# First loads of a hybrid decoder step put on one DMA queue in small pieces, and the square root's activation table loaded behind a square

## The chip, the cores and the metric

The kernel runs on one core of a Trainium2 chip. A core has five engines that run side by side, each with an instruction queue of its own: TensorE (PE, with its weight loads shown as PEld), VectorE (DVE), ScalarE (ACT), GpSimd (POOL) and SyncE (SP, which only issues transfers). ACT and POOL can issue transfers too; each issuing engine has a DMA queue, and all queues run on the same 16 DMA engines. The metric is the device time of one execution in microseconds (us), lower is better.

## The reference, cut to what matters

The reference is one layer of a hybrid decoder for 256 prompt tokens and 8 x 8 sample tokens (320 in all, width 2048), in fp32:

```
h    = rms_norm(x, norm_mix_pre)
proj = h @ w_in                                  # 2048 x 9248
a_u, a_v, z, xbc, dt_raw = split(proj)
gate = chunk_spatial_gate(a_u, a_v, ...)         # gelu, layer norm, masked 128x128 mix per head
ssm  = ssd_mixer(z, xbc, dt_raw, ...)            # causal conv, silu, chunked state space scan, group rms norm
x    = x + rms_norm(concat(gate, ssm) @ w_out, norm_mix_post)
up   = causal_conv(rms_norm(x, norm_ffn_pre) @ ffn_w_up)
x    = x + rms_norm((gelu_tanh(g) * u) @ ffn_w_down, norm_ffn_post)    # g, u = halves of up
```

with `rms_norm(x, w) = x * rsqrt(mean(x*x) + 1e-6) * w`. The new convolution and state-space states are outputs as well.

## The kernel before

All activations are kept with the model width on the 128 partitions and the 320 tokens along the free dimension: x is `xT`, 16 k-tiles of 128 x 320, behind 16 columns that hold the first norm's weights.

**Matmuls.** Each weight block is split into a rounded part `whi` and a rest `wlo`, and each activation into `h_hi` and `h_lo`; `accumulate` (L126) makes three matmuls of them, 128 x 128 by 128 x 320 each: hi x hi, hi x lo, lo x hi. `slab` (L110) loads a piece of a weight matrix into `wraw` on SP's queue (L115), casts it to `whi` on ACT (L117) and subtracts on DVE (L119) to make `wlo`. `wraw`, `whi` and `wlo` have three buffers each, so the load of a slab waits until the third slab before it has been split, and a cast waits until TensorE is done with the third slab before it.

**project** (L152) multiplies the 2048 rows of a weight matrix by 512 (or 256) of its columns. Its list `cuts` runs over the k-tiles: with `small=4` the first four slabs hold one k-tile x 512 columns (256 KB), the next four hold two k-tiles (512 KB), and the last four k-tiles come as two slabs of 256 columns. For each cut it calls `ready(k0, nk)`, if there is one, and then `part`, which calls `slab`, the matmuls and one `tick`. `tick` (L140) advances the background tasks in `bg` by one yield.

**The start.** The first projection (columns V0 to V0 + 511) has `ready=x_ready`. `x_ready` (L525) makes `h_hi` on ACT (L529) and `h_lo` on DVE (L530) from x, scaled by the norm's weights alone: the factor 1/rms, `r1`, is multiplied in when a result leaves PSUM, so the matmuls needn't wait for it. x comes by six transfers that ACT issues ahead of everything (L516 to L518; 1, 1, 2, 4, 4 and 4 k-tiles), with a small square between them (L521) that loads ACT's table early. Before its first real matmul TensorE runs `EARLY` = 10 matmuls of ones (L69).

The sums of squares for `r1` need x once more, with the tokens on the partitions: `load_by_token` (L540) issues six transfers of `x_tok` on POOL's queue, four of 512 KB and two of 256 KB. In front of each, POOL copies one column of `h_hi` of k-tile 8 into the destination, which keeps the transfer behind that k-tile. `x_squares` (L546) squares each piece on ACT with an accumulated sum (L549); each is queued behind one of the last h_hi operations on ACT. The task `with_r1` (L570) has a yield, then `x_squares` and the reciprocal root on DVE, a yield, then `spread` (TensorE turns the column into a row), the parameter loads, and the evacuations `late` of the first projection (`scaled`: DVE multiplies by r1, L334, ACT takes the gelu, L335). It is started once and then advanced by the ticks of the second projection, V0 + 512, 256 columns wide. `turned` (L555) transposes the results on TensorE (`vt_ps`).

**The two later roots.** The mixer's output (`chunk_out(w_out, 7, ...)`, L987) and the FFN's output (`chunk_out(ffn_w_down, g, ...)` with the last g, L1137) are summed up in 16 blocks of 128 x 320. `squares_of` (L284) gives the callback that squares each block as it is finished: blocks 0 to 12 by `add_square` (L276: square on ACT, sum on POOL), 13 to 15 at high priority with the sum on DVE. After the last block `token_sums` adds over the partitions and `rsqrt_by_root` (L237) takes `Sqrt` on ACT (L245), whose table is not the one that gelu, silu and exp use. `root_table` (L252) issues a `Sqrt` of one column whose result nobody reads, so that the table is there beforehand. It is called ahead of each of the two last `chunk_out`s with the last matmul of the chunk before them (L984, L1136).

**Order.** The order of instructions on each engine is set when the program is built, by readiness in a model and by priority: `tc.high_priority(offset=...)` moves what it encloses forward, `first()` being the 200000 step, and a slab's load has 100000. `tc.issue_after(ins)` queues what is traced inside it behind `ins`, as far as it is on the engine of `ins`.

Of the kernel before, what the change touches and what calls it, by code (L numbers as in the profile page):

```python
# [9 lines left out]
F32 = mybir.dt.float32  # L10
F32R = mybir.dt.float32r
I32 = mybir.dt.int32
AF = mybir.ActivationFunctionType
ALU = mybir.AluOpType
# [3 lines left out]
P = 128  # L18
# [3 lines left out]
NT = NP + NS  # L22
D = 2048
KD = D // P
# [1 line left out]
NF = DFF // P  # L26
NH = 32
EPS = 1e-6
EARLY = 10
D_COL = 4 * KD + 120 + 8 * NF  # L30
U0, V0, Z0, X0, B0, C0, DT0 = 0, 2048, 4096, 6144, 8192, 8704, 9216

# [2 lines left out]
def hybrid_step(  # L35
# [10 lines left out]
    act, dve, pool, pe, sp = nc.scalar, nc.vector, nc.gpsimd, nc.tensor, nc.sync  # L46
# [6 lines left out]
    tp = ctx.enter_context(tc.tile_pool(name="tp", bufs=2))  # L53
# [10 lines left out]
    ones = cp.tile([P, P], F32, name="ones")  # L64
# [70 lines left out]
    hT = [None, None]  # L135
# [60 lines left out]
    acc = None  # L196
    pd_last = []
# [54 lines left out]
    def root_table(behind):  # L252

        there = tp.tile([P, 1], F32, name="root_there", bufs=1)
        with tc.issue_after(behind):
            act.activation(there, ones[:, 0:1], AF.Sqrt)
# [18 lines left out]

    def add_square(total, x, begins, adder=pool, place=("sq", 2)):  # L276
        if begins:
            act.activation(total, x, AF.Square)
        else:
            sq = tp.tile([P, NT], F32, tag=place[0], name="sq", bufs=place[1])  # L280
            act.activation(sq, x, AF.Square)
            adder.tensor_tensor(out=total, in0=total, in1=sq, op=ALU.add)

    def squares_of(total):  # L284

        one, held = [], []

        def step(nb):
            if nb < KD - 3:
                add_square(total, acc[:, nb, :], nb == 0)  # L290
                return
            with first():
                if nb < KD - 1:
                    held.append(misc("sq_ps")[:, :NT])
                else:
                    one.append(tp.tile([P, NT], F32, tag="sq", name="sq", bufs=2))
                act.activation((one or held)[-1], acc[:, nb, :], AF.Square)
                if nb > KD - 3:
                    dve.tensor_tensor(out=total, in0=total, in1=held.pop(0), op=ALU.add)
        return step, one  # L300
# [10 lines left out]
    acc = hp.tile([P, KD, NT], F32, name="acc_mix")  # L311
# [50 lines left out]
    with ExitStack() as mctx:  # L362
        op = mctx.enter_context(tc.tile_pool(name="op", bufs=1))
# [138 lines left out]
        with tc.tile_pool(name="gp", bufs=1) as gp:  # L502
# [3 lines left out]
            flat = vt.rearrange("p c d -> p (c d)")  # L506
# [4 lines left out]
            wS = gp.tile([P, 4, NB, TS], F32, name="wS")  # L511
            pool.memset(wS[NS:], 0.0)
            held = gp.tile([P, 1], F32, name="held")
            k = 0
            with tc.high_priority(offset=300000):
                for n in (1, 1, 2, 4, 4, 4):  # L516
                    cs = slice(KD + NT * k if k else 0, KD + NT * (k + n))
                    act.dma_start(flat[:, cs], xT[:, cs])  # L518
                    k += n
                    if k == 2:  # L520
                        act.activation(held, ones[:, 0:1], AF.Square)  # L521

            x_split = []

            def x_ready(k0, nk):  # L525
                with tc.high_priority(offset=100000):
                    for kt in range(k0, k0 + nk):
                        x = xf[:, kt, :]
                        x_split.append(act.activation(hT[0][:, kt, :], x, AF.Copy, scale=pre[:, kt:kt + 1]).ins)  # L529
                        dve.scalar_tensor_tensor(out=hT[1][:, kt, :], in0=x, scalar=pre[:, kt:kt + 1],  # L530
                                                 in1=hT[0][:, kt, :].bitcast(F32), op0=ALU.mult, op1=ALU.subtract)
# [5 lines left out]
            by_tok = [(xp[:, c, D // 2 * i:D // 2 * (i + 1)], slice(0, P), slice(P * c, P * c + P), c, i)  # L537
                      for c in range(2) for i in range(2)]
            by_tok += [(t.rearrange("p k n -> p (k n)")[64:, :D // 2], slice(64, P), slice(NP, NT), 2, i) for i, t in enumerate((bT, cT))]
            def load_by_token():  # L540
                for t, _, rows, c, i in by_tok:

                    pool.tensor_copy(t[:, 0:1], hT[0][:, 8, 0:1][t.shape[0] % P:].bitcast(F32))
                    pool.dma_start(t, x_tok[rows, D // 2 * i:D // 2 * (i + 1)])

            def x_squares():  # L546
                for n, (t, at, _, c, i) in enumerate(by_tok):
# [17 lines left out]

            late = []
            project(w_in, V0, lambda j, ps: scaled(ps, AF.Gelu, vfs[0][:, j, :]), ready=x_ready, small=4, ahead=0, late=late)
            load_by_token()

            def with_r1():  # L570
                yield
                with first():
                    r = x_squares()
                yield
                spread(r, r1)
                params()
                for ev, j, ps in late:
                    ev(j, ps)
# [107 lines left out]
        with tc.tile_pool(name="sd", bufs=1) as sd:  # L686
# [294 lines left out]
            finish(norm3)  # L981
            sq2 = hp.tile([P, NT], F32, tag="ssq", name="sq2")

            root_table(pd_last[-1])  # L984
            bg.append(islice(rest[0], 3))
            squares, one = squares_of(sq2)
            chunk_out(w_out, 7, *res[3], False, squares)  # L987
# [50 lines left out]
    with tc.tile_pool(name="fp", bufs=1) as fp:  # L1038
# [90 lines left out]
        for g in range(NG):  # L1129
            hi, lo = nxt  # L1130
            if g < NG - 1:
                nxt = ffn_up(g + 1)
            if g == 0:
                acc = fp.tile([P, KD, NT], F32, name="acc_ffn")
            if g == NG - 1:
                root_table(pd_last[-1])  # L1136
            chunk_out(ffn_w_down, g, hi, lo, g == 0, last if g == NG - 1 else None)  # L1137

        act.dma_start(o_fconv_p, ptf)
# [125 lines left out]
```

## Time and profile before

| | |
|---|---|
| median of 3 runs | 1821.66 us (1821.31 to 1822.76) |
| span of the profiled execution | 1821.3 us |
| TensorE busy | 1789.4 us, 98% of the span |
| VectorE, ScalarE, GpSimd busy | 1182.3, 798.1, 304.5 us |
| moved by DMA | 294.66 MB, mean 162 GB/s |

The profile is of one execution. Times in it count from the start of the span. A timeline row has the start, the duration, the engine, the line, the operation and what it writes and reads (`out<-in`), with the count of merged operations; in brackets stands the idle time of the engine just ahead of it and what ended it. ACTq, SPq and POOLq are the rows in which an engine issues transfers. Queue q1 is SP's, q10 ACT's and q0 POOL's. Matmuls overlap, so the distance between two starts, not the duration, is what one costs.

### The profile page before, as it was taken

The numbers are of one execution on the slowest core, as the hardware profiler recorded it, in microseconds if no ns is written. First come the engines' busy times: TensorE is split into PE (matmuls) and PEld (weight loads), VectorE is DVE, ScalarE is ACT, GpSimd is POOL, SyncE is SP. The second block draws the span as 40 slices with busy tenths as digits, with TensorE's granted clock in tenths as the row PEclk, the third lists the DMA queues.
The fourth block names the chain that finished last, engine by engine and source line by source line (L and its number), as shares of the span: only waits on it lengthen the run. The fifth ranks groups of instructions, "written<-read, shape, count | busy, mean of one in ns | idle before, by whom it ended". The sixth has DMA issues, their size and how long they took to land.

```text
span 1821.3 us, 31186 instructions
## 1 busy us (share of the span) xinstructions
PE 1789.4 (98%) x12222; PEld 1751.6 (96%) x12222; DVE 1182.3 (65%) x2029; ACT 798.1 (44%) x1102; POOL 304.5 (17%) x626
## 2 busy tenths in 40 slices
PE   8999999999999999999899999999999999999998
PEld 8999999999889899999899999999999999999997
DVE  5449664557977868677776465647465665756575
ACT  6444454334535445444455433333334343433334
POOL 3102200000331312104521010101111010101004
PEclk9999999999999999999999999999999999999999
DMA  8656544455566565556454545444545445454542
GB/s 268 186 150 189 159 132 152 155 157 176 189 192 189 162 196 173 156 159 206 148 149 151 150 153 153 151 152 151 153 152 154 150 154 150 151 148 153 151 154 99
DMA packets 222947, 294.66 MB, mean 162 GB/s; under 512 B 16752, under 2 KB 150736, under 8 KB 222608
## 3 DMA queue, kind: packets, MB, share of 16 engines
q1 hardware_dynamic: 210544, 270.21, 48.6%
q10 hardware_dynamic: 9872, 14.82, 2.2%
q0 software_dynamic: 2384, 7.64, 1.4%
q8 instruction: 96, 1.57, 0.4%
q14 instruction: 51, 0.42, 0.1%
HBM read 277.80 MB, written 14.82 MB: 161 GB/s over the span
## 4 chain that ended last, share of the span: by engine, by line
PE 88%; DVE 4%; DMA 2%; issue 2%; POOL 2%; ACT 1%; ACTq 0%; POOLq 0%; DVEq 0%
PE ps L128 18%; PE ps L130 18%; PE ps L129 18%; PE pd L128 9%; PE pd L130 9%; PE pd L129 9%; DVE wlo L119 1%; PE y_ps L888 1%; DMA cT<-in_x_tok 1%; POOL acc_mix L1023 1%; ACT whi L117 1%; DMA cs<-dacs_d 1%; DMA st<-in_state_ssm 0%; POOL st L808 0%; PE sg L650 0%
## 5 line engine op out<-in xcount | busy, mean ns | idle before, releaser
L119 DVE TENSOR_TENSOR wlo<-wraw,whi 128x1024 fp32r<-128x1024 f32 (+1 forms) x476 | 592.0, 1244 | 455.4 <-ACT whi L117 452.8
L117 ACT CAST whi<-wraw 128x1024 fp32r<-128x1024 f32 (+1 forms) x476 | 496.3, 1043 | 730.2 <-PE ps L129 443.7
L128 PE MATMUL ps<-h_hi,whi 128*128 128x320 f32 x2528 | 787.5, 312 | 8.6 <-ACT whi L117 5.6
L130 PE MATMUL ps<-h_hi,wlo 128*128 128x320 f32 x2528 | 783.9, 310 | 4.3 <-DVE wlo L119 4.3
L129 PE MATMUL ps<-h_lo,whi 128*128 128x320 f32 x2528 | 782.8, 310 | 0.0
L128 PEld LDWEIGHTS ps<-h_hi,whi 128*128 128x128 f32 x2528 | 477.5, 189 | 14.2 <-ACT whi L117 6.9
L130 PEld LDWEIGHTS ps<-h_hi,wlo 128*128 128x128 f32 x2528 | 477.2, 189 | 6.6 <-DVE wlo L119 6.4
L129 PEld LDWEIGHTS ps<-h_lo,whi 128*128 128x128 f32 x2528 | 477.5, 189 | 0.7 <-issue 0.5
L128 PE MATMUL pd<-fhi,whi 128*128 128x320 f32 x704 | 217.0, 308 | 0.0
L129 PE MATMUL pd<-flo,whi 128*128 128x320 f32 x704 | 217.0, 308 | 0.0
L130 PE MATMUL pd<-fhi,wlo 128*128 128x320 f32 x704 | 217.0, 308 | 0.0
L128 PE MATMUL pd<-ohi,whi 128*128 128x320 f32 x448 | 140.8, 314 | 0.0
L129 PE MATMUL pd<-olo,whi 128*128 128x320 f32 x448 | 139.5, 311 | 0.0
L130 PE MATMUL pd<-ohi,wlo 128*128 128x320 f32 x448 | 139.4, 311 | 0.0
L128 PEld LDWEIGHTS pd<-fhi,whi 128*128 128x128 f32 x704 | 132.1, 188 | 0.0
L129 PEld LDWEIGHTS pd<-flo,whi 128*128 128x128 f32 x704 | 132.1, 188 | 0.0
L130 PEld LDWEIGHTS pd<-fhi,wlo 128*128 128x128 f32 x704 | 132.1, 188 | 0.0
L1074 POOL COPY ptf<-pad 128x2 f32<-128x2 f32 x88 | 20.5, 233 | 618.1 <-DVE pad L1062 617.4
L211 DVE TENSOR_TENSOR acc_ffn<-acc_ffn,pd 128x320 f32<-128x320 f32 x160 | 77.5, 484 | 38.7 <-PE pd L130 37.4
L128 PEld LDWEIGHTS pd<-ohi,whi 128*128 128x128 f32 x448 | 84.8, 189 | 2.9 <-issue 1.6
L130 PEld LDWEIGHTS pd<-ohi,wlo 128*128 128x128 f32 x448 | 84.7, 189 | 1.0 <-issue 1.0
L129 PEld LDWEIGHTS pd<-olo,whi 128*128 128x128 f32 x448 | 84.8, 189 | 0.5 <-issue 0.2
(297 smaller groups left out, 1599.4 us busy)
## 6 DMA issues: line engine op xcount, KB each, us to landing
wraw<-in_ffn_w_up SPq DMA_DIRECT2D x176, 512.0 KB, 3.7
wraw<-in_w_in SPq DMA_DIRECT2D x144, 512.0 KB, 3.7
wraw<-in_ffn_w_down SPq DMA_DIRECT2D x88, 512.0 KB, 3.5
wraw<-in_w_out SPq DMA_DIRECT2D x64, 512.0 KB, 3.5
st<-in_state_ssm SPq DMA_DIRECT2D x40, 256.0 KB, 3.8
out_ssm_state_sample<-st ACTq DMA_DIRECT2D x30, 256.0 KB, 3.6
cs<-dacs_d SPq DMA_DIRECT2D x16, 320.0 KB, 4.3
xr<-in_xT SPq DMA_DIRECT2D x4, 640.0 KB, 4.8
```

The source lines that it names most:

```text
L117: act.copy(hi[:, :m], raw[:, :m])
L119: dve.tensor_tensor(out=lo[:, :m], in0=raw[:, :m], in1=hi[:, :m].bitcast(F32), op=ALU.subtract)
L128: pe.matmul(ps, whi, xhi, start=first, stop=False)
L129: pe.matmul(ps, whi, xlo, start=False, stop=False)
L130: return pe.matmul(ps, wlo, xhi, start=False, stop=last).ins
L211: dve.tensor_tensor(out=acc[:, nb, :], in0=acc[:, nb, :], in1=ps[:, :NT], op=ALU.add)
L888: pe.matmul(ps[64 * i:64 * i + 64, cols], w(hl), x(hl, m, cpx), tile_position=(0, 64 * i), **flags)
L1023: added.append((dve if kt < 2 else pool).tensor_tensor(out=a, in0=a, in1=xr[q][:, k, :], op=ALU.add).ins)
L1074: pool.tensor_copy(ptf[:, k, :], pad[:, 256:258])
```

## The change

x is no longer issued by ACT: `x_ready` issues each cut's x on SP's queue, at the priority of the slabs and ahead of the cut's own slab in the text: pieces of 1, 1, 1, 1, 2, 2, 2, 2 and 4 k-tiles. The token loads go to SP as well, one behind the x of k-tile 8, one behind that of 10, two behind that of 12, and the last two behind the first projection; POOL's small copies are gone. `with_r1` has one yield more at its head. `EARLY` is 8.

`add_square` and the callback of `squares_of` now hand over the square's instruction, and the callback calls `root_table` behind the square of block 12 (`nb == KD - 4`), the last that `add_square` makes; the two earlier calls are gone.

```diff
-EARLY = 10
+EARLY = 8
...
     def add_square(total, x, begins, adder=pool, place=("sq", 2)):
         if begins:
-            act.activation(total, x, AF.Square)
-        else:
-            sq = tp.tile([P, NT], F32, tag=place[0], name="sq", bufs=place[1])
-            act.activation(sq, x, AF.Square)
-            adder.tensor_tensor(out=total, in0=total, in1=sq, op=ALU.add)
+            return act.activation(total, x, AF.Square).ins
+        sq = tp.tile([P, NT], F32, tag=place[0], name="sq", bufs=place[1])
+        made = act.activation(sq, x, AF.Square).ins
+        adder.tensor_tensor(out=total, in0=total, in1=sq, op=ALU.add)
+        return made
...
         def step(nb):
             if nb < KD - 3:
-                add_square(total, acc[:, nb, :], nb == 0)
+                made = add_square(total, acc[:, nb, :], nb == 0)
+                if nb == KD - 4:
+                    root_table(made)
                 return
...
-            k = 0
             with tc.high_priority(offset=300000):
-                for n in (1, 1, 2, 4, 4, 4):
-                    cs = slice(KD + NT * k if k else 0, KD + NT * (k + n))
-                    act.dma_start(flat[:, cs], xT[:, cs])
-                    k += n
-                    if k == 2:
-                        act.activation(held, ones[:, 0:1], AF.Square)
+                act.activation(held, ones[:, 0:1], AF.Square)
...
             def x_ready(k0, nk):
                 with tc.high_priority(offset=100000):
+                    cs = slice(KD + NT * k0 if k0 else 0, KD + NT * (k0 + nk))
+                    sp.dma_start(flat[:, cs], xT[:, cs])
+                    for _ in range({8: 1, 10: 1, 12: 2}.get(k0, 0)):
+                        load_by_token()
                     for kt in range(k0, k0 + nk):
...
+            to_load = list(by_tok)
+
             def load_by_token():
-                for t, _, rows, c, i in by_tok:
-
-                    pool.tensor_copy(t[:, 0:1], hT[0][:, 8, 0:1][t.shape[0] % P:].bitcast(F32))
-                    pool.dma_start(t, x_tok[rows, D // 2 * i:D // 2 * (i + 1)])
+                if to_load:
+                    t, _, rows, _, i = to_load.pop(0)
+                    sp.dma_start(t, x_tok[rows, D // 2 * i:D // 2 * (i + 1)])
...
-            load_by_token()
+            with tc.high_priority(offset=100000):
+                while to_load:
+                    load_by_token()
 
             def with_r1():
+                yield
                 yield
...
-            root_table(pd_last[-1])
             bg.append(islice(rest[0], 3))
             squares, one = squares_of(sq2)
             chunk_out(w_out, 7, *res[3], False, squares)
...
-            if g == NG - 1:
-                root_table(pd_last[-1])
             chunk_out(ffn_w_down, g, hi, lo, g == 0, last if g == NG - 1 else None)
```

## The prediction

> **What bounds the kernel now.** I read the page first (busy shares, chain of waits), then windows over the start, then the timeline of each engine at the start and at the two places where a square root is taken.
>
> ```profile
> span 1821.3 us, 31186 instructions
> PE 1789.4 (98%) x12222; PEld 1751.6 (96%) x12222; DVE 1182.3 (65%) x2029; ACT 798.1 (44%) x1102; POOL 304.5 (17%) x626
> PE 88%; DVE 4%; DMA 2%; issue 2%; POOL 2%; ACT 1%; ACTq 0%; POOLq 0%; DVEq 0%
> ```
>
> TensorE is busy for 98% of the span and carries 88% of the chain. A change that leaves its work alone can win only where it idles or runs slowly, so I looked for those places inside the stages that are edited. The windows have the columns length, then busy time and count of PE, PEld, DVE, ACT and POOL, then granted clock, DMA share, GB/s.
>
> ```profile
> 5.70:42.25 36.55, 31.98 (x194) 30.02 (x195) 20.41 (x39) 25.23 (x41) 9.14 (x16) 0.95 0.89 285
> ...
> 26.00:29.21 3.21, 3.21 (x14) 3.21 (x13) 0.55 (x2) 2.28 (x5) 0.00 (x0) 0.50 1.08 206
> 42.25:56.67 14.42, 14.42 (x102) 14.40 (x101) 8.03 (x10) 8.98 (x14) 4.67 (x8) 1.00 0.71 206
> ```
>
> The first projection has 16 k-tiles x 4 blocks x 3 = 192 matmuls. From 42.25 TensorE runs without a gap: about 96 matmuls and a few transposes in 14.42 us, so 0.147 us each, or 28.2 us for 192. The first 192 took from 5.72 to about 42.1, 36.4 us: **8.2 us are lost** after the first matmul. The rows below show where.
>
> ```profile
> 1.13 4.54 PE L70 MATMUL early<-ones 128*128 128x128 f32 x20 [1.13 <-DVE ones L66]
> ...
> 5.72 0.41 PE L128 MATMUL ps<-h_hi,whi 128*128 128x320 f32 x1
> ```
> ```profile
> 11.40 0.31 PE L130 MATMUL ps<-h_hi,wlo 128*128 128x320 f32 x1
> 12.77 0.41 PE L128 MATMUL ps<-h_hi,whi 128*128 128x320 f32 x1 [1.07 <-ACT whi L117]
> ```
> ```profile
> 22.61 0.31 PE L130 MATMUL ps<-h_hi,wlo 128*128 128x320 f32 x1
> 24.47 0.41 PE L128 MATMUL ps<-h_hi,whi 128*128 128x320 f32 x1 [1.55 <-ACT whi L117]
> 24.72 0.31 PE L129 MATMUL ps<-h_lo,whi 128*128 128x320 f32 x1
> 25.73 0.48 PE L130 MATMUL ps<-h_hi,wlo 128*128 128x320 f32 x1 [0.70 <-DVE wlo L119]
> ```
>
> Start to start, the gap at 12.77 costs 1.37 - 0.15 = 1.2 us, the one at 24.47 costs 1.86 - 0.15 = 1.7, the one at 25.73 costs 1.01 - 0.15 = 0.9. Behind them the granted clock is 0.50 for 3.2 us: some 13 matmuls at 0.27 instead of 0.147, 1.6 us. These are 5.4 of the 8.2; the rest is handed over in pieces of 0.1 to 0.7 us while hi and lo halves are made.
>
> Who is late at 12.77 and 24.47? Rows of SP's issues, of the queues' shares at 7.7 to 9.0, of landing times, and of ACT:
>
> ```profile
> 1.73 0.43 SPq L115 DMA_DIRECT2D wraw<-in_w_in  x1
> 6.42 0.33 SPq L115 DMA_DIRECT2D wraw<-in_w_in  x1
> ```
> ```profile
> q10 hardware_dynamic: 116, 0.54, 100.5%
> ```
> ```profile
> wraw<-in_w_in SPq DMA_DIRECT2D x1, 256.0 KB, 5.6
> ```
> ```profile
> 22.33 1.06 ACT L549 ACTIVATE acc_mix<-acc_mix 128x1024 f32<-128x1024 f32 x1 [4.98 <-DMA acc_mix<-in_x_tok]
> 23.29 0.19 ACT L549 ACTIVATION_READ_ACCUMULATOR acc_mix<-acc_mix 128x1 f32 x1
> 23.39 1.03 ACT L117 CAST whi<-wraw 128x1024 fp32r<-128x1024 f32 x1
> ```
>
> The fourth slab is issued at 6.42 (raw slabs have three buffers) and lands 5.6 us later, since ACT's queue, q10, holds all of the engines with x that is needed much later. At 22.33 ACT has stood 4.98 us for x by token, which POOL fetched, and the cast that TensorE needs stands behind that square. Both are what an order of loads can cure.
>
> **The change part by part.** *Loads.* Six transfers of x leave ACT's queue and become nine, six token loads leave POOL's; all go to SP, between the slabs. The bytes stay: x 320 x 2048 x 4 = 2.62 MB, the same again by token, weights 2048 x 512 x 4 = 4.19 MB. Can one queue carry it, and soon enough?
>
> ```profile
> 2.50:14.00 11.50, 10.05 (x57) 9.06 (x56) 6.87 (x15) 7.66 (x16) 2.97 (x15) 1.00 1.02 403
> 14.00:18.00 4.00, 3.63 (x25) 3.37 (x24) 3.76 (x6) 3.35 (x6) 3.94 (x8) 1.00 0.66 182
> 18.00:33.00 15.00, 12.75 (x75) 12.22 (x74) 4.29 (x6) 8.31 (x13) 1.64 (x4) 0.89 1.01 287
> 36.50:38.70 2.20, 1.72 (x12) 1.46 (x10) 2.06 (x7) 2.14 (x5) 0.21 (x1) 1.00 1.08 396
> ```
>
> From 36.50 on only SP's queue has work (the slab and the parameters), and it moves 396 GB/s; two queues moved 403. An issue takes SP about 0.4 us (1.73 row), so fifteen more take 6 us of a sequencer that is otherwise waiting. In the order of use a k-tile costs (160 + 256) KB = 0.426 MB, 1.06 us at 403 GB/s, against 12 x 0.147 = 1.76 us of TensorE. With the four token loads placed among them, all that must land before the first of the last two slabs is used is 2.62 + 2.10 + 3.67 = 8.39 MB: 2.5 + 8.39/0.403 = 23.3 us, plus about 1.0 for the cast, 24.3. TensorE would want it at 4.9 + 12 x 1.76 = 26.0. It fits, with 1.7 us to spare. The x pieces now stand behind slabs that wait for a raw buffer; a buffer comes free when its lo half is made, long before TensorE needs the x of three slabs later, so I count nothing for that. Left over I put 0.6 us for the first halves, 0.3 for other hand-overs and 1.0 for a slab that arrives late: 1.9 of the 8.2, so **-6.3 us**. The bounds are 0 (all of it comes back) and -8.2 (none).
>
> *The first matmul.* The ten warm-up matmuls take 4.54 us, 0.454 each; eight end at 1.13 + 3.63 = 4.76. Today the first cast ends at 5.67 behind two transfers (x on ACT's queue, the slab on SP's) that share the engines with their successors. With x and slab first on one queue, 424 KB need 1.05 us at 403 GB/s, behind a start at about 2.5; ACT then needs about 1.1 for h_hi and the cast, 4.7. I take 4.9: **-0.8 us**, bounds 0 and -0.95.
>
> *POOL.* Six small copies and six issues go; POOL is idle before and behind them in that stretch, so 0.
>
> *One more yield.* The spread of r1 and the four late evacuations come one slab later, 24 x 0.147 = 3.5 us.
>
> ```profile
> 54.03 1.19 ACT L335 ACTIVATE vf<-ev 128x320 f32<-128x320 f32 x3
> ```
> ```profile
> 56.51 1.47 PE L561 MATMUL vt_ps<-ident,vf 128*128 128x128 f32 x12
> ```
>
> The last of these gelus ends at 55.22 and the transposes that read them start at 56.51: 1.3 us of cover. One slab later they would be 2.2 us late, if the transposes keep their place. But the order of an engine is made by readiness:
>
> ```profile
> 4.87 0.10 POOL L594 MEMSET mv<- 128x6 f32 x1
> ```
>
> This memset stands in the text behind four projections and runs at 4.87. Matmuls of the next projection can go first in the same way, so I take 0 and keep +2.2 for the range.
>
> *The square root's table.* Today the helper asks to be put behind a matmul, an instruction of another engine, and what it issues is on ACT:
>
> ```profile
> 36.89 1.28 ACT L256 ACT_TABLE_LOAD   x1
> 38.18 0.44 ACT L256 ACTIVATE root_there<-ones 128x1 f32<-128x1 f32 x2
> ```
>
> Both dummies ran at 38.2, long before a root. The real roots then loaded again:
>
> ```profile
> 857.39 1.28 ACT L245 ACT_TABLE_LOAD   x1
> ...
> 858.29 0.16 DVE L244 SCALAR_TENSOR_TENSOR rs_v<-tsum,rs_v 128x3 f32<-128x3 f32 x1 [0.44 <-PE tsum L263]
> 858.68 0.20 ACT L245 ACTIVATE rs_s<-rs_v 128x3 f32<-128x3 f32 x1
> ```
> ```profile
> 1804.43 0.56 ACT L1125 ACTIVATE acc_ffn<-acc_ffn,prm 128x320 f32<-128x320 f32 x1
> ...
> 1805.01 1.28 ACT L245 ACT_TABLE_LOAD   x1
> ...
> 1805.32 0.16 DVE L244 SCALAR_TENSOR_TENSOR rs_v<-tsum,rs_v 128x3 f32<-128x3 f32 x1 [1.17 <-PE tsum L263]
> 1806.31 0.20 ACT L245 ACTIVATE rs_s<-rs_v 128x3 f32<-128x3 f32 x1
> ```
>
> Behind a square, an ACT instruction, the dummy holds its place, and no gelu, silu or exp stands between it and the root. At the end the operand is ready at 1805.48 and the root starts at 1806.31; without the load it starts at about 1805.52: **-0.8**. In the middle: 858.45 to 858.68, **-0.2**. The load moves to 1.28 + 0.2 = 1.5 us after the square of block 12:
>
> ```profile
> 1798.65 0.47 ACT L281 ACTIVATE sq<-acc_ffn 128x320 f32<-128x320 f32 x1 [0.69 <-DVE acc_ffn L211]
> ...
> 1800.35 0.44 ACT L297 ACTIVATE sq_ps<-acc_ffn 128x320 f32<-128x320 f32 x1 [0.63 <-DVE acc_ffn L211]
> ```
>
> That ends at 1800.6, so the next square is 0.3 late; the scaled copies are pushed too, and the last square (1803.9) comes 3 us later, time enough. Without this cover the load would cost its 1.3 us again. The load at 36.89 goes for nothing gained; TensorE's next wait is for a lo half whose cast (ACT, just ahead of the load) was done by then:
>
> ```profile
> 38.76 0.41 PE L130 MATMUL ps<-h_hi,wlo 128*128 128x320 f32 x1 [0.54 <-DVE wlo L119]
> ```
>
> The Trainium skill, "ScalarE: Activation LUTs", section "What ACT_TABLE_LOAD costs", gives a switch as 1.28 us of load plus 1.38 us of drain, which by estimate would make the two gains together up to 2.8 larger, 1810.8 in all. Here the load starts 0.02 us after the operation before it and the root 0.02 behind the load, so no drain lies there and I leave it out.
>
> The sum: -6.3 - 0.8 - 0.8 - 0.2 = -8.1 us; 1821.3 - 8.1 = 1813.2 of span. The median of the runs, 1821.66, is 0.36 over the span, so **1813.6 us**.
>
> **The rivals.** *Run-ahead.* The x and token pieces wait for nothing, the slabs from the fourth on do. If readiness orders SP as it orders POOL, pieces are issued while a slab waits, and the slab stands behind them in the same queue. Up to the fourth slab some 2 us are open, four to five issues, and so on at each slab; in the end all x, all tokens and the weights up to k-tile 9 (2.62) land first, 7.86 MB: 2.5 + 7.86/0.403 + 1.0 = 23.0, where k-tile 8 is wanted at 4.9 + 8 x 1.76 = 19.0. 4.0 us are lost instead of the 1.0 that I put: 1816.6, and with a stretch at half clock like that at 26.00 (1.6) 1818.2. The memset row speaks for it; against it, that only a few pieces fit into each wait.
>
> The Trainium skill, "DMA: Bandwidth & Descriptors", section "Queues, rings and completion order", has each DMA engine take turns between the queues that hold work. By this rule a slab on a queue of its own gets its share at once, which one queue gives away, so it speaks against the change; and the gap at 12.77 (1.2 us) would not come from x, which would leave 1814.8. The row of q10 disagrees: 100.5% for ACT's queue at 7.7 to 9.0, with SP's slab issued at 6.42.
>
> *The start stays as it is.* ACT takes things strictly in its order; if a square again stands ahead of a cast and its tokens land late (the 4.98 us at 22.33), the gap, the half clock after it and so most of the 8.2 us return, and the tail's 1.0 is all: 1820.7. The token loads on a fast queue ahead of their slabs speak against it.
>
> *Slower: one queue is too slow.* The 8.9 MB that must land before the last slab is cast went, today, in time for a start at about 38.6. They need 2.5 + 8.9/rate + 1.0; below 8.9/35.1 = 254 GB/s the start is slower than before. At 206 GB/s (the 26.00 row) the last slab comes at 46.7, 8 us late: 1821.7 + 8 - 1 = 1828.7. For it: 182 GB/s at 14.00 to 18.00, where SP had few transfers under way. Against it: 396 at 36.50.
>
> **How the numbers follow.** Forecast (1811 to 1815.5) 0.52; run-ahead (1815.5 to 1818.6) 0.25; start unchanged (1820 to 1822) 0.17, with the case that the late evacuations eat what a half-cured start wins; one queue too slow 0.06. What a measurement here can tell from no change is about 0.2%, 3.6 us, so faster means below 1818.0: 0.52 + 0.23 = 0.75; same 0.19; slower 0.06. The range: from 1810.8 (nothing left of the 8.2, first matmul at 4.76) to 1818.8, which takes in run-ahead and leaves out unchanged and slower, 0.2 in all.
>
> **What would show it.** Right: the first matmul near 4.9, the end of the first projection near 35, no stretch at half clock, no wait of ACT for tokens ahead of a cast; one table load in front of a dummy in each of the two last chunks and none at the root. Wrong: token issues ahead of the fourth or fifth slab on SP, a matmul waiting 2 us or more for a cast between 10 and 24, the twelve transposes late, or a load left at the root.

## The result, and the profile after

| | before | after |
|---|---|---|
| median of 8 runs each, same chip | 1821.99 us (1821.31 to 1823.06) | 1816.53 us (1814.83 to 1819.09) |
| ratio | | 0.9971, 95% interval [0.9961, 0.9981] |
| span of the profiled execution | 1821.3 us | 1815.3 us |
| first matmul | 5.72 | 4.80 |
| extra time of the first projection | 8.2 us | 4.0 us |

5.5 us were gained (3.5 to 7.1 by the interval); 8.1 were forecast, as 1813.6 us. The time lies in the range of 1810.8 to 1818.8, but outside the 1811 to 1815.5 that the forecast itself was given 0.52 for.

The head of the page and of the chain of waits after, for comparison with those of before:

```profile
span 1815.3 us, 31168 instructions
...
PE 1785.2 (98%) x12218; PEld 1747.4 (96%) x12218; DVE 1180.9 (65%) x2028; ACT 796.4 (44%) x1101; POOL 299.4 (16%) x614
...
PE 83%; issue 6%; DVE 4%; DMA 3%; POOL 1%; ACT 1%; SPq 0%; ACTq 0%; POOLq 0%; DVEq 0%
```

TensorE is still the bound; it has lost 4.2 us of busy time, two warm-ups and the stretch at half clock among them. The windows of the start after (same columns as in the prediction):

```profile
2.50:14.00 11.50, 9.93 (x61) 9.06 (x60) 6.46 (x13) 6.89 (x13) 3.66 (x14) 1.00 0.96 306
14.00:18.00 4.00, 4.00 (x27) 3.92 (x28) 4.00 (x6) 3.71 (x6) 0.00 (x0) 1.00 1.03 408
18.00:33.00 15.00, 14.40 (x99) 14.14 (x97) 7.49 (x11) 10.75 (x19) 1.80 (x1) 1.00 1.05 312
...
27.00:33.00 6.00, 5.40 (x37) 5.14 (x36) 2.85 (x4) 4.76 (x9) 1.80 (x1) 1.00 1.09 220
```

The clock is 1.00 in every row. But one queue moved 306 GB/s in the first window, where two had moved 403, and only 220 at 27 to 33, although the engines show as fully taken (share 1.09). TensorE's gaps after, from its timeline, and the two casts on ACT that they wait for:

```profile
4.80 0.41 PE L128 MATMUL ps<-h_hi,whi 128*128 128x320 f32 x1 [0.27 <-ACT whi L117]
...
12.25 0.31 PE L130 MATMUL ps<-h_hi,wlo 128*128 128x320 f32 x1
13.86 0.41 PE L128 MATMUL ps<-h_hi,whi 128*128 128x320 f32 x1 [1.30 <-ACT whi L117]
...
31.50 0.31 PE L130 MATMUL ps<-h_hi,wlo 128*128 128x320 f32 x1
32.41 0.41 PE L128 MATMUL ps<-h_hi,whi 128*128 128x320 f32 x1 [0.60 <-ACT whi L117]
...
33.67 0.42 PE L130 MATMUL ps<-h_hi,wlo 128*128 128x320 f32 x1 [0.40 <-DVE wlo L119]
```
```profile
12.77 1.04 ACT L117 CAST whi<-wraw 128x1024 fp32r<-128x1024 f32 x1 [2.11 <-DMA wraw<-in_w_in]
...
31.32 1.04 ACT L117 CAST whi<-wraw 128x1024 fp32r<-128x1024 f32 x1 [1.02 <-DMA wraw<-in_w_in]
```

Start to start, less 0.147 for the matmul itself, the gaps cost 1.46 (slab of k-tile 4), 0.76 and 0.56 (second slab of the last four k-tiles). Together with some 0.55 of small hand-overs at the first k-tiles and 0.7 of smaller ones around the named gaps and at the next slab they make 4.05 us, where before had 8.18. Both casts waited for a slab in flight; no cast stands behind a square that waits more than 0.2 us for its tokens.

The roots. ACT's rows (the square ahead of each load, the load, the dummy, the root), and the rows of DVE and PE behind the last root, after and then before:

```profile
845.83 1.28 ACT L256 ACT_TABLE_LOAD   x1
...
1793.18 0.47 ACT L280 ACTIVATE sq<-acc_ffn 128x320 f32<-128x320 f32 x1 [0.43 <-POOL sq L281]
1793.67 1.28 ACT L256 ACT_TABLE_LOAD   x1
1794.96 0.20 ACT L256 ACTIVATE root_there<-ones 128x1 f32<-128x1 f32 x1
...
1799.67 1.86 PE L1148 MATMUL x1p<-acc_mix,ident 128*128 128x320 f32 x6
1799.85 0.16 DVE L244 SCALAR_TENSOR_TENSOR rs_v<-tsum,rs_v 128x3 f32<-128x3 f32 x1 [1.17 <-PE tsum L263]
1800.04 0.20 ACT L245 ACTIVATE rs_s<-rs_v 128x3 f32<-128x3 f32 x1 [0.52 <-DVE rs_v L244]
...
1801.37 0.82 PE L271 MATMUL spread<-ident,rs_r 128*128 128x128 f32 x6
```
```profile
1805.14 1.86 PE L1147 MATMUL x1p<-acc_mix,ident 128*128 128x320 f32 x6
...
1807.15 0.16 DVE L249 SCALAR_TENSOR_TENSOR rs_r<-rs_t,rs_r 128x3 f32<-128x3 f32 x1
1807.37 0.87 PE L271 MATMUL spread<-ident,rs_r 128*128 128x128 f32 x6 [0.36 <-DVE rs_r L249]
```

No load is left at a root; the last root starts 0.03 after its operand (1800.01), before it was 0.83. But the spread behind it no longer waits for DVE: it now stands behind the six x1p matmuls, which end at 1801.53. So of the 0.80 gained at the root, the span's end sees less. With the trace's times unrounded, from the start of L244 to the end of the span it was 1821.334 - 1805.317 = 16.02 us, and is 1815.266 - 1799.845 = 15.42, a gain of **0.60**.

### The profile page after: what moved, and what is told of

Its sections match the earlier page's. It is cut to its first block, busy times and chain, and to the rows that moved or that the text cites. A ratio compares the mean times of both kernels' runs of the same rounds, so it can differ in the third digit from the quotient of the medians.

```text
span 1815.3 us, 31168 instructions
## 1 busy us (share of the span) xinstructions
PE 1785.2 (98%) x12218; PEld 1747.4 (96%) x12218; DVE 1180.9 (65%) x2028; ACT 796.4 (44%) x1101; POOL 299.4 (16%) x614
## 4 chain that ended last, share of the span: by engine, by line
PE 83%; issue 6%; DVE 4%; DMA 3%; POOL 1%; ACT 1%; SPq 0%; ACTq 0%; POOLq 0%; DVEq 0%
PE ps L128 17%; PE ps L130 17%; PE ps L129 17%; PE pd L128 10%; PE pd L130 9%; PE pd L129 9%; DMA wraw<-in_w_in 1%; DVE wlo L119 1%; PE y_ps L892 1%; POOL acc_mix L1026 1%; DMA st<-in_state_ssm 1%; ACT whi L117 1%; DMA cs<-dacs_d 1%; PE sg L654 0%; DVE cv L388 0%
```

## The experiments

All are compared with the kernel before on the same chip, in runs of their own. Single runs of one kernel spread by 2 to 9 us, so variants that lie within 2 us of each other are told apart by their profile, not by their time. The table has for each the ratio and two sums from the starts of TensorE's matmuls: the extra time over 0.1468 us per matmul (their mean distance where nothing is waited for) up to the 145th matmul (before the last slabs of the first projection) and up to the 230th (behind the first slab of the next).

| kernel | median, us | ratio to before | extra to 145 | extra to 230 |
|---|---|---|---|---|
| before | | 1 | 7.3 | 8.2 |
| after | 1816.53 | 0.9971 [0.9961, 0.9981] | 2.2 | 4.0 |
| a1, root part alone | 1821.12 | 1.0001 [0.9993, 1.0010] | 7.3 | 8.5 |
| a2, loads alone | 1815.79 | 0.9969 [0.9956, 0.9981] | 1.6 | 4.3 |
| a3, larger pieces of x | 1814.36 | 0.9962 [0.9949, 0.9975] | 2.6 | 4.0 |
| a4, last slabs in rows of 2 KB | 1815.45 | 0.9971 [0.9962, 0.9980] | 3.0 | 5.5 |
| b1, x issued by ACT | 1821.31 | 1.0000 [0.9991, 1.0010] | 7.4 | 9.2 |
| b2, tokens last | 1817.92 | 0.9986 [0.9975, 0.9997] | 0.9 | 4.3 |
| b3, ten warm-ups | 1815.83 | 0.9976 [0.9967, 0.9985] | 2.5 | 3.6 |
| b4, one yield | 1814.59 | 0.9965 [0.9952, 0.9977] | 1.9 | 4.0 |
| c1, 128 rows for 64 | 1813.51 | 0.9956 [0.9941, 0.9971] | 2.7 | 3.8 |
| c4, two slabs more under way | 1815.48 | 0.9965 [0.9955, 0.9976] | 1.2 | 5.9 |
| d1, c4 and one load of 128 half rows | 1822.21 | 1.0004 [0.9996, 1.0013] | 1.4 | 11.0 |
| d2, d1 with one yield | 1821.89 | 1.0001 [0.9992, 1.0010] | 1.3 | 11.0 |

### The two halves of the change

a1 is the kernel before with the new `add_square` and its call of `root_table`; a2 is the kernel after with the two old calls of `root_table` and without the new one.

> The kernel before with only the root's table moved behind the square of block 12. Theory (the load is on the path at the two roots only): no table load at either root, the last root starts 0.03 us behind its operand, and the time is 0.8 to 1.0 us under before, about 1821.0. Rival (the new place of the load shifts the order elsewhere and that carries part of the 5.5 us): 1819.5 or less, or no change.

> The changed kernel with the two calls of the root's helper put back as before. Theory: the loads carry all but 0.8 to 1.0 us of the gain, so about 1817.4, with both table loads back at the roots. Rival (the table carries nothing that shows): 1816.5.

Instructions by line, a1 (loads behind the square, L256) and a2 (loads at the root, L245); then a2's first matmul:

```profile
L256 ACT ACT_TABLE_LOAD  x2: 1283/1283/1283, 850.5 to 1797.4; - x2
```
```profile
L245 ACT ACT_TABLE_LOAD  x2: 1283/1283/1283, 851.5 to 1797.8; - x2
```
```profile
5.25 0.42 PE L128 MATMUL ps<-h_hi,whi 128*128 128x320 f32 x1 [0.61 <-ACT whi L117]
```

The loads carry the gain: a2's ratio is that of after (the two times expected for a2, 1817.4 and 1816.5, lie too near each other for its 1815.79 to choose). The root part alone can't be told from nothing by its time (-1.3 to +1.8 us by its interval). The profiles tell it: from L244's start to the end of the span a1 takes 15.42 us, like after (15.42), and a2 16.00, like before (16.02). So these 0.6 us belong to the table load, in both pairs.

### Why one queue moves 300 GB/s at the start

a3 loads x in pieces of 1, 1, 2, 4, 4 and 4 k-tiles on SP; a4 cuts the last four k-tiles into slabs of two k-tiles x 512 columns:

```diff
-                    cs = slice(KD + NT * k0 if k0 else 0, KD + NT * (k0 + nk))
-                    sp.dma_start(flat[:, cs], xT[:, cs])
+                    n = {0: 1, 1: 1, 2: 2, 4: 4, 8: 4, 12: 4}.get(k0, 0)
+                    if n:
+                        cs = slice(KD + NT * k0 if k0 else 0, KD + NT * (k0 + n))
+                        sp.dma_start(flat[:, cs], xT[:, cs])
```
```diff
-            while k0 < KD - 4:
+            while k0 < KD - tail:
```

> The changed kernel with x in pieces of 1, 1, 2, 4, 4, 4 k-tiles instead of 1, 1, 1, 1, 2, 2, 2, 2, 4, still on SP's one queue. In the changed kernel the engines move 300 GB/s from 3 to 13 us where before they moved 403, and TensorE waits 1.5 us for the slab of k-tile 4. Theory (short rows in small x pieces set that rate): 380 GB/s or more from 3 to 13, no wait at k-tile 4, about 1815.0. Rival (one queue is slower than two, whatever the pieces): 300 GB/s stays, the wait stays or grows by the 0.8 us that the longer piece of x ahead of the slab takes, 1816.5 to 1817.3.

> The changed kernel with the last four k-tiles of the first projection as two slabs of 2 k-tiles x 512 columns (rows of 2 KB) instead of 4 k-tiles x 256 columns (rows of 1 KB). In the changed kernel the engines move 220 GB/s from 27 to 33 us and TensorE loses 1.7 us between 31.5 and 34. Theory (the 1 KB rows set that rate): 350 GB/s or more there and no wait for the last slabs, about 1814.8. Rival (the slabs are late because the token loads stand ahead of them in the queue): the waits stay, 1816.5.

The window 3 to 13 of a3 and 27 to 33 of a4:

```profile
3.00:13.00 10.00, 9.09 (x53) 8.27 (x53) 5.95 (x12) 5.86 (x12) 3.37 (x13) 1.00 0.90 292
```
```profile
27.00:33.00 6.00, 5.56 (x38) 5.29 (x37) 2.24 (x2) 2.64 (x6) 0.00 (x0) 1.00 1.08 240
```

Neither size is the cause, so both theories missed: 292 GB/s with larger pieces of x (after: 301), and 240 with the first projection's last rows twice as long (after: 220).

b1 gives the pieces of x to ACT again, c4 lets two slabs more be under way:

```diff
-                    sp.dma_start(flat[:, cs], xT[:, cs])
+                    act.dma_start(flat[:, cs], xT[:, cs])
```
```diff
-            raw = wp.tile([P, 1024], F32, tag="wraw", name="wraw", bufs=3)
+            raw = spare_raw.pop(0) if spare_raw else wp.tile([P, 1024], F32, tag="wraw", name="wraw", bufs=3)
...
+            spare_raw += [acc.rearrange("p k n -> p (k n)")[:, 2 * D + 512 * i:2 * D + 512 * (i + 1)] for i in range(2)]
```

> As after, but the nine pieces of x are issued by ACT; weights and tokens stay on SP, where the two first token loads now come ahead of the fourth slab. Theory (one queue that alternates rows of 1.3 KB and 2 KB moves about 300 GB/s, two move 400): between 3 and 13 us at least 380 GB/s in place of 301, first matmul at 4.8 to 5.3. If only the rate mattered, the 1.30 us wait at 12.25 to 13.86 would be gone; but if a slab behind token loads is late (the rival named in the prediction, run-ahead), it stays or grows to 1.5 us or more, now because of 1 MB of tokens in front of the slab. Rival (one queue is as fast as two, the 301 is a lack of work): the rate stays below 330. Extra time of the first projection: 2.5 us by the first theory, 4 or more by run-ahead; time 1815 or 1817.

> As after, but the first two slabs go to a piece of the accumulator that is free then, so that the three raw buffers serve the slabs from the third on: two slabs more can be under way. The fourth to sixth slabs are then issued 2 to 4 us earlier (5.50, 7.02 and 9.04 in after). Theory (the 301 GB/s at 3 to 13 come from too little work in the queue, since SP stands at the raw buffers): the rate at 3 to 13 rises to 350 or more, no wait of 0.5 us or more between 10 and 16 (1.46 in after), extra time of the first projection about 2.6 in place of 4.04. Rival (one queue that alternates short pieces of x and slabs gives 300 whatever is waiting in it): the rate stays below 320, slabs land when they did, and the wait at 12 to 14 stays at 0.8 or more.

For b1 the window, TensorE's longest gap and the cast behind it:

```profile
3.00:13.00 10.00, 9.48 (x44) 8.94 (x44) 4.56 (x10) 4.20 (x8) 2.15 (x11) 1.00 1.01 358
```
```profile
33.95 1.01 PE L128 MATMUL ps<-h_hi,whi 128*128 128x320 f32 x3 [3.09 <-ACT h_hi L529]
```
```profile
32.39 1.04 ACT L117 CAST whi<-wraw 128x1024 fp32r<-128x1024 f32 x1 [5.39 <-DMA wraw<-in_w_in]
```

Two queues moved 358, not the 380 expected, and it was no use: the extra time is 9.2 us, and all that the change had won is gone (ratio 1.0000). With x gone from SP, token loads stand ahead of the fourth slab, as in the run-ahead of the prediction, but that slab (issued at 6.36, landed 5.4 us later) is not what TensorE waits for. Of the 9.2 us, 2.3 lie at the start, where 15 matmuls come 0.267 us apart, although the granted clock is recorded as 1.00; 3.3 are the gap shown; and 1.8 follow it, most of them at a granted clock of 0.54 (33.9 to 37.4). In the gap TensorE waits for the `h_hi` of the last piece of x. ACT issues that piece at 22.90, behind its casts, it lands 9.1 us later, and its `h_hi` stands on ACT behind the cast shown, whose slab is issued at 21.73 and lands 10.6 us later. One token load is issued ahead of that slab (20.55) and one of 64 rows behind it (22.15), which is the matter of the next section. So b1 shows that x on ACT's queue wins nothing, but not what run-ahead alone costs.

For c4 the window and the gap of the last slab:

```profile
3.00:13.00 10.00, 9.01 (x54) 8.30 (x54) 6.73 (x13) 7.27 (x13) 3.63 (x13) 1.00 0.99 329
```
```profile
31.37 0.31 PE L130 MATMUL ps<-h_hi,wlo 128*128 128x320 f32 x1
33.49 0.42 PE L128 MATMUL ps<-h_hi,whi 128*128 128x320 f32 x1 [1.81 <-ACT whi L117]
```

329 GB/s lies between the two expectations (350 and more, below 320). The two kernels d1 and d2 below share the edit and moved 343 and 338, and all variants with x on SP and three raw buffers 278 to 309: so too few slabs under way are a part of the cause, and the rest stays open. The gap at 12 to 14 is gone in c4, d1 and d2; but it is also missing in a2 and b2, which don't share the edit, so this says little. What c4 doesn't wait for at k-tile 4 it waits for at the last slab (2.0 in place of 0.76), in a stretch that moves 210 GB/s (27 to 33), and behind that wait the granted clock is 0.51 from 35.2 to 38.6, which costs another 1.5 us.

### The loads to half of the partitions

b2 puts all six token loads behind the weights of the first projection:

```diff
-                    for _ in range({8: 1, 10: 1, 12: 2}.get(k0, 0)):
-                        load_by_token()
```

> As after, but none of the six token loads stands among the pieces of x and the slabs: all follow the weights of the first projection. Theory (the two waits of the last slab, 0.76 and 0.56 at 31.5 to 33.0, come from 2.6 MB of tokens that are in front of it on the one queue): the last slab lands 4 us or more earlier, both waits are below 0.2, extra time of the first projection about 2.5 in place of 4.04. The wait at 12.25 (1.30), which lies ahead of most tokens, stays. Rival (1 KB rows make the last slabs slow): the waits stay at 0.5 or more. The squares of x by token come later, and what waits for r1 with them: the transposes at about 52 to 57 or the evacuations may be 0 to 3 us later. Time 1815 if that is hidden, 1817 or more if not.

```profile
37.59 0.31 PE L130 MATMUL ps<-h_hi,wlo 128*128 128x320 f32 x1
39.69 0.41 PE L128 MATMUL ps<-h_hi,whi 128*128 128x320 f32 x1 [1.78 <-ACT whi L117]
...
41.70 0.42 PE L130 MATMUL ps<-h_hi,wlo 128*128 128x320 f32 x1 [1.17 <-DVE wlo L119]
```
```profile
37.28 1.05 ACT L548 ACTIVATE cT<-cT 64x1024 f32<-64x1024 f32 x1 [0.48 <-DMA cT<-in_x_tok]
38.59 1.04 ACT L117 CAST whi<-wraw 128x1024 fp32r<-128x1024 f32 x1 [0.16 <-DMA wraw<-in_w_in]
```

The first projection now runs with 0.9 us lost in all, so the two waits of the last slab do come from the token loads. In after four of them are issued ahead of that slab (19.48), and the first one of 64 rows just behind it (19.95). But the slab of the next projection pays: its cast stands behind the last square on ACT, and TensorE waits 1.95 + 1.32 us. The sum is the same 4.3.

In b2 too the rate falls to about half for some 5 us, only later, at 30 to 35 (140 to 200 GB/s). In the packet records of after, from 28 to 35, a row of 4 KB takes 250 to 420 ns (the median of each us), and ahead of that 159; a row of 1 KB in the same queue takes 70 to 115 ns, and ahead of that 46. In before, after and b2 the rows of 4 KB in the slow stretch number some 110 to 130: they fit the two times 64 rows of the last 64 tokens, which go to partitions 64 to 127. In before these loads are on POOL's queue, and the slabs' rows of 1 KB on SP's queue take 79 to 98 ns at 26 to 30 all the same, so the slowed rows need not be in the same queue. c1 loads 128 rows in their place, to all partitions, the same rows of 4 KB and twice the bytes:

```diff
-            to_load = list(by_tok)
+            to_load = by_tok[:4] + [(t.rearrange("p k n -> p (k n)")[:, :D // 2], None, slice(NT - P, NT), 2, i) for i, t in enumerate((bT, cT))]
```

> As after, but the two loads that put 64 rows of x by token on partitions 64 to 127 take 128 rows each and fill all partitions: the same rows of 4 KB, twice the bytes (0.52 MB more); the rows that were not needed are not read. Theory (a load to 64 partitions runs at half the rate and slows the slabs that share the queue: 220 GB/s at 27 to 33 with a share of 1.09): the rate at 27 to 33 rises to 350 or more, the two waits of the last slab (0.76 and 0.56 at 31.5 to 33.0) fall to 0.2 or less together although more bytes move, extra time of the first projection about 2.7 in place of 4.04; time up to 1.3 us better. Rival (the slabs' rows of 1 KB are the slow part, or simply too many bytes are ahead): the rate stays at 200 to 250, the slab lands later still, by 0.5 MB / 220 GB/s = 2.4 us, and the waits grow to 2 us or more.

The window of c1, then the landing of the first of the two loads in after and in c1 (KB, and us from issue to landing):

```profile
27.00:33.00 6.00, 5.60 (x38) 5.29 (x37) 3.33 (x5) 5.98 (x12) 1.81 (x1) 1.00 1.06 377
```
```profile
bT<-in_x_tok SPq DMA_DIRECT2D x1, 256.0 KB, 12.6
```
```profile
bT<-in_x_tok SPq DMA_DIRECT2D x1, 512.0 KB, 10.9
```

377 GB/s in place of 220, with 0.52 MB more to move, and twice the bytes land sooner. So the loads of 64 rows to half of the partitions were slow, and they slowed the slabs beside them; in c1 a row of 4 KB takes 161 to 173 ns in that stretch, and a row of 1 KB 46 to 51. It wasn't the slabs' rows of 1 KB, which are the same in c1, nor where the tokens lie in memory, since c1 reads the same rows too. c1 changes the number of rows together with the partitions; 64 rows spread over both halves, in a form that all 16 engines share, were not run. The Trainium skill, "SBUF — State Buffer", section "Door 1: The DMA port swizzle", says that what counts is how many of 16 ports a transfer's partitions reach, and by its table 64 to 127 reach eight, so half the rate; the trace agrees, 220 against 377. The prediction did not weigh this rule. It bears on before as well, which has the same loads and a slow stretch of its own at 26 to 31.

The time follows only in part. ACT and DVE of c1 at the last slabs, and TensorE:

```profile
30.36 1.04 ACT L550 ACTIVATE acc_mix<-acc_mix 128x1024 f32<-128x1024 f32 x1
31.40 1.03 ACT L117 CAST whi<-wraw 128x1024 fp32r<-128x1024 f32 x1
```
```profile
32.46 1.23 DVE L119 TENSOR_TENSOR wlo<-wraw,whi 128x1024 fp32r<-128x1024 f32 x1 [1.42 <-ACT whi L117]
```
```profile
33.74 0.41 PE L130 MATMUL ps<-h_hi,wlo 128*128 128x320 f32 x1
```

No transfer ends ACT's idle time any more: it has none, the cast at 31.40 starts as the square ends. TensorE's gaps at the last slabs are 0.56 and 0.30, both waits for a lo half behind a cast behind a square. ACT, with six squares of 1.05 us to fit between the casts, is the next bound, close behind the queue: before this it had stood 1.77 us for the last piece of x, at 25.50. From the 145th matmul on, c1 loses 1.1 us in place of 1.85. The whole extra time fell only from 4.0 to 3.8, since c1 lost 0.5 more ahead of that, in the first 16 us, where it is the same kernel. The two waits, expected at 0.2 or less together, were 0.56 and 0.30. c1's median is the best of all, 1813.51, but its interval overlaps with that of after.

### Warm-ups and the extra yield

b3 has `EARLY = 10`, b4 one of the two yields.

> As after, with ten warm-up matmuls in place of eight. The prediction's step: with ten the warm-up ends at 5.4 (two more of 0.45, from 4.53), and the first matmul starts at 5.45 to 5.5 in place of 4.80, with no wait for ACT; after that the waits shrink by some of the 0.65, since the loads get ahead by it (the wait at 12.25 from 1.30 to about 0.65). Net time of the first projection's end 0 to 0.7 later. Rival (the first matmul is set by the cast whatever the warm-up): 4.80 to 5.0.

> As after, with one yield ahead of the work on r1 as in the kernel before. The prediction counted the second yield at nothing, with +2.2 us as its upper end. Theory (r1 comes as late as its tokens; the extra yield takes nothing from the transposes): the wait ahead of the transposes of the value half stays within 0.3 us of after's (0.2 at 52.4, 0.40 at 67.9), but with one yield TensorE may meet the spread of r1 before its operand is there, a new wait of 0.5 to 2 us at about 40 to 45. Rival (the extra yield costs): the transposes come without a wait and the shift at 57 us is 0.3 to 2 us better. Time 1816.5 or 1815.5.

```profile
1.13 4.02 PE L70 MATMUL early<-ones 128*128 128x128 f32 x20 [1.13 <-DVE ones L66]
5.02 0.42 PE L128 MATMUL ps<-h_hi,whi 128*128 128x320 f32 x1
```

In b3 no wait for ACT is left ahead of the first matmul, so there the warm-ups set it, but at 5.02 and not at 5.45: ten took 4.02 us in this execution and 4.54 in before. With eight, the first matmul came between 4.76 and 5.25 in the runs that keep x on SP, in half of them with a wait for the first cast. So the two warm-ups are worth some tenths, and a single trace can't give more. The wait at k-tile 4 did not shrink as expected: it cost 1.45 in b3, and 1.46 in after. In b4 TensorE doesn't meet the spread at 40 to 45, and the transposes have no gap, where after has waits for the gelu of 0.19 at 52.4 and 0.40 at 67.9. From the 230th matmul to the 600th after takes 59.7 us and b4 58.9, as before does. c4, which has both yields but comes later to this stretch, takes 58.9 too. So the extra yield seems to cost up to 0.8 us where TensorE comes early.

### Both cures together

d1 joins c4 with another form of the token load: the 64 tokens come in one transfer onto 128 partitions, half a row each (no bytes more, one square fewer on ACT), and a small copy brings the two sums together. d2 has one yield besides.

```diff
+                        sp.dma_start(t, x_tok[rows, :].rearrange("t (h d) -> h t d", h=2))
...
+                    sp.dma_start(ssq[64:, 2, 1:2], ssq[:64, 2, 0:1])
```

> As after, with the first two slabs in a free piece of the accumulator (as in the run with more raw slabs under way) and the last 64 tokens loaded once, onto all 128 partitions (first half of their columns on partitions 0 to 63, second half on 64 to 127, the two sums of squares brought together by a small copy); one square fewer on ACT, the bytes are those of after. Theory (the two causes of the 4.04 us are separate: raw buffers at 12 to 14, loads to 64 partitions at 31 to 34): no wait of 0.5 us or more between 10 and 16, at least 350 GB/s at 27 to 33, no wait of 0.5 us or more between 31 and 34, extra time of the first projection 1.5 to 2.2, time about 1813. Rival (what is saved at one slab is waited for at the next, since the queue is always behind): extra time stays at 3.5 or more, with the waits at another slab; time about 1815.

> As the run before it, with one yield ahead of the work on r1. If the extra yield costs nothing (the prediction's step), the waits ahead of the transposes of the value half stay below 0.3 us in both, and the two times are within 1 us of each other. Rival (r1 asked for one slab earlier is not there yet, since the small copy adds some 2 us): a new wait of 0.5 to 2 us of TensorE at 38 to 45.

Windows of d1, TensorE's one long gap and the ACT row that ends it:

```profile
4.80:34.20 29.40, 29.04 (x192) 28.50 (x192) 17.90 (x27) 19.37 (x32) 3.21 (x7) 1.00 0.91 321
```
```profile
33.00:37.00 4.00, 1.53 (x11) 1.27 (x9) 0.00 (x0) 0.00 (x0) 0.00 (x0) 1.00 0.13 51
```
```profile
34.22 0.31 PE L130 MATMUL ps<-h_hi,wlo 128*128 128x320 f32 x1
40.95 0.64 PE L128 MATMUL ps<-h_hi,whi 128*128 128x320 f32 x1 [6.42 <-ACT whi L117]
```
```profile
38.36 1.06 ACT L553 ACTIVATE bT<-bT 128x1024 f32<-128x1024 f32 x1 [8.37 <-DMA bT<-in_x_tok]
```

The whole first projection runs in 29.4 us for 192 matmuls, 1.4 lost and none of it behind k-tile 1: nothing holds TensorE there but the first casts. Then it waits 6.4 us, because the square of the new load stands ahead of the next cast and its data are not there. The load moves 51 GB/s with a share of 0.13, two of sixteen engines. The Trainium skill, "DMA: Bandwidth & Descriptors", section "Why a DMA increments its semaphore by 16 and not by 1", lets the slowest dimension of a transfer that isn't 1 decide how many engines share it, here h = 2; the trace agrees. So both expectations missed, theory and rival: the waits of the first projection went, and a new, larger one came from the form in which the load was written. Behind it the granted clock is 0.50 from 41.3 to 46.5; that and the matmuls just ahead of it are the other 3 us of the 11.0. d2 is the same to 0.3 us; what it asked is hidden by that wait. A form with 128 partitions outermost was not tried, and whether both cures together would beat c1 stays open.

## Why the prediction was right, and where its size was off

- **The first matmul, -0.8:** it came 0.92 earlier. Right, within the few tenths by which this point moves from run to run.
- **Order on SP:** right. SP issues pieces and slabs in the order of the text, and each token load one slab later than in the text (the first at 10.73, behind the slab of k-tile 8 at 10.31); no token goes ahead of the fourth or fifth slab, and no cast waits for tokens. The time of 1816.5 is that of the rival run-ahead by accident only: the order that it supposes isn't there.
- **The first projection, -6.3:** the mechanism held (no half clock, no cast behind a square that lacks its tokens), the size did not: 8.18 - 4.05 = **4.13 us**. The term that was mis-sized is what is left over, 1.9 in the prediction and 4.05 measured. Hand-overs and first halves were 1.3 where I put 0.9. "1.0 for a slab that arrives late" was 1.46 at k-tile 4 and 0.76 + 0.56 at the last slab. Behind it stands the step "2.5 + 8.39/0.403 = 23.3 us", all bytes at the rate of two queues: one queue moved 301 at 3 to 13 and 220 at 27 to 33. The slab for which that sum was made, the first of the last two, landed at 25.5 and was not waited for. The late ones are the slab of k-tile 4, for which no sum was made, and the second of the last two, at which the sum stops short. The rate of 220 is the loads to half of the partitions (c1). The row of 206 GB/s at 26.00, quoted in the prediction, was this effect already; I used it as a rate that one queue might have, and did not ask which transfers were under way in it. For the 301 the size of the pieces of x is excluded (a3), and more slabs under way raise it only to 329 to 343 (c4, d1 and d2).
- **Where the last part is bound:** ACT's squares were not in the sum at all. b2 and c1 show that with the transfers out of the way the casts wait behind them.
- **The tail, -0.8:** right at the root, 0.60 at the end of the span, since the x1p matmuls were next; the question "what is late next" was not asked there. **The root in the middle, -0.2:** there the root follows its operand at once after, so 0.2 of waiting went, too little for any run to show by its time.
- **The extra yield, 0:** up to 0.8 against the change (b4), inside the +2.2 that I kept for the range. **POOL, 0:** nothing in the profile speaks against it.

In sum -0.92 - 4.13 + 0.8 - 0.60 - 0.2 = -5.05, beside 6.07 by the spans and 5.5 by the medians. The missing 1.0 lies between the 600th matmul (at 102 to 109 us) and the last, where nothing but the root in the middle was edited: before takes 1696.4 us there, after 1695.2, and the other kernels 1691.5 (d2) to 1696.6 (b3). So a single profile can't carry the sum to better than some us, and that it comes near the medians is partly luck.

## What to carry to other kernels

Price a queue by what is in it, stretch by stretch, and not by its best rate: a window with a full DMA share and half of the usual GB/s names a transfer, and its partitions and its outermost dimension are the first things to look at. When several engines feed one in-order consumer, a saved wait moves to the next slab until the total load of the queue or the engine (here SP's bytes, then ACT's squares) is less, so sum up to a point behind the whole stage, not to the gap that closed.

## What was not expected of the hardware

- A load of 64 rows to partitions 64 to 127 slows the transfers beside it by about half, in its own queue (after) and in another (before): rows of 1 KB take 70 to 115 ns in place of 46, and all together moves 220 GB/s, against 377 with 128 rows.
- A transfer with an outermost dimension of 2 moved 51 GB/s.
- One queue with slabs and pieces of 160 to 640 KB moved 278 to 309 GB/s at 3 to 13 in all variants with x on SP and three raw buffers; two queues in before moved 410. The median row of 2 KB takes 84 ns in both; in after 7 to 13% of these rows take more than 1.5 times that in most slices of 1 us, in before at most 3%. Why is open.
- Behind waits of TensorE of 2.0 us (c4), 3.3 (b1) and 6.6 (d1) the granted clock was 0.50 to 0.54 for 3.4 to 5.2 us; behind 1.95 + 1.32 us in b2 it stayed at 1.00.
